# A batched matmul with stores six batches behind the loads, copies of two banks and a small first store

## The chip, the cores and the metric

The kernel runs on one core of a Trainium2 chip. The metric is the device time in microseconds (us), the median of several runs. The profile page describes one execution, and that one has a time of its own.

## The reference

```python
def setup_inputs():
    batch, m, k, n = 16, 512, 512, 512
    return {
        "a": np.random.randn(batch, k, m).astype(np.float32),
        "b": np.random.randn(batch, k, n).astype(np.float32),
    }

def reference(a: np.ndarray, b: np.ndarray) -> np.ndarray:
    return np.matmul(a.transpose(0, 2, 1), b).astype(np.float32)
```

There are 16 independent products of 512x512 matrices, the first one transposed. Each matrix is 1 MB (1,048,576 bytes) in float32, so the kernel must read 32 of them and write 16.

## The kernel before

A batch is one unit of work. Its matrix `a` (512 rows of k by 512 columns of m) lies in SBUF as a tile of 128 partitions, with four consecutive rows of k in each partition. So a partition's part of a batch is one run of 8 KB in memory, and a batch's `a`, `b` and output are each one DMA of 128 such runs. `load(i)` (L45) issues the DMAs of `a` (L46) and `b` (L47), and `store(i)` (L49) the one of the output (L50). All of them are issued by SyncE, SP in the profile, so they stand in one queue.

`compute(i)` (L52) has three steps:

- VectorE (DVE) casts `a` and then `b` from float32 to bfloat16 (L55, L56), 128x2048 each.
- TensorE (PE) makes the output in four groups, one for each `mo`. A group is four matmuls of 128x512 (L61) that are summed in one PSUM bank. The eight banks, `ps0` to `ps7`, are used in turn, so a batch takes four and the next batch the other four.
- ScalarE (ACT) copies each bank to a quarter of the output tile (L68), 128x512 at a time. Its table load before the first copy has the same line.

The buffers are five tiles each of `a` and `b` (`NL`), three of each cast (`NB`), and six output tiles (`NO`), all used in turn. A step that would overwrite a buffer waits until the readers of its former content are done; Tile sets these waits. For its DMAs from SP and ACT, Tile also has eight semaphores that it hands out in turn in the order of the program. A DMA waits until the eighth before it, which had the same semaphore, has landed. So no more than eight are under way at a time.

What sets the order on SP's queue is the loop at the end (L70 to L76): four batches are loaded ahead, and then for each batch come the load of the batch four further on, the computing, and its store. SP issues in that order, and while it waits for one instruction, all behind it wait too. In SP's order the transfers are: ten loads (batches 0 to 4), the store of batch 0, the loads of batch 5, the store of batch 1, and so on. The last load is the 43rd of 48, and the stores of batches 11 to 15 follow it.

Of the kernel before, what the change touches and what calls it, by code (L numbers as in the profile page):

```python
# [1 line left out]

# [4 lines left out]

@with_exitstack
def kernel(
    ctx: ExitStack,  # L10
    tc: tile.TileContext,
    a: bass.AP,
    b: bass.AP,
    out: bass.AP,
):
    nc = tc.nc
    P = 128
    batch, K, M = a.shape
    _, _, N = b.shape
    KO = K // P  # L20
    MO = M // P
    f32 = mybir.dt.float32
    bf = mybir.dt.bfloat16

    a_v = a.rearrange("bat (ki ko) m -> bat ki ko m", ko=KO)
    b_v = b.rearrange("bat (ki ko) n -> bat ki ko n", ko=KO)
    out_v = out.rearrange("bat (mi mo) n -> bat mi mo n", mo=MO)

    LAG = 4
    NL = LAG + 1
    NB = 3
    NO = LAG + 2

    pool = ctx.enter_context(tc.tile_pool(name="sb", bufs=1))
    psum = ctx.enter_context(tc.tile_pool(name="ps", bufs=1, space=bass.MemoryType.PSUM))
    a_ts = [pool.tile([P, KO, M], f32, name=f"a{j}") for j in range(NL)]
    b_ts = [pool.tile([P, KO, N], f32, name=f"b{j}") for j in range(NL)]
    abf_ts = [pool.tile([P, KO, M], bf, name=f"abf{j}") for j in range(NB)]  # L40
    bbf_ts = [pool.tile([P, KO, N], bf, name=f"bbf{j}") for j in range(NB)]
    o_ts = [pool.tile([P, MO, N], f32, name=f"o{j}") for j in range(NO)]
    ps_ts = [psum.tile([P, N], f32, name=f"ps{j}") for j in range(8)]

    def load(i):  # L45
        nc.sync.dma_start(a_ts[i % NL][:], a_v[i])  # L46
        nc.sync.dma_start(b_ts[i % NL][:], b_v[i])  # L47

    def store(i):  # L49
        nc.sync.dma_start(out_v[i], o_ts[i % NO][:])  # L50

    def compute(i):  # L52
        af, bff = abf_ts[i % NB], bbf_ts[i % NB]
        o = o_ts[i % NO]
        nc.vector.tensor_copy(out=af[:], in_=a_ts[i % NL][:])  # L55
        nc.vector.tensor_copy(out=bff[:], in_=b_ts[i % NL][:])  # L56
        a_m = af[:].rearrange("p ko (mi mo) -> p ko mo mi", mo=MO)
        for mo in range(MO):
            pt = ps_ts[(i * MO + mo) % 8]
            for ko in range(KO):  # L60
                nc.tensor.matmul(  # L61
                    pt[:],
                    a_m[:, ko, mo, :],
                    bff[:, ko, :],
                    start=(ko == 0),
                    stop=(ko == KO - 1),
                )
            nc.scalar.copy(out=o[:, mo, :], in_=pt[:])  # L68

    for i in range(min(LAG, batch)):  # L70
        load(i)
    for i in range(batch):
        if i + LAG < batch:
            load(i + LAG)
        compute(i)
        store(i)  # L76


# [1 line left out]
_INS = ['a', 'b']  # L80
_OUTS = [((16, 512, 512), 'float32')]


# [23 lines left out]
```

## Time and profile before

| | |
|---|---|
| Time, median of 5 runs | 126.16 us (125.88 to 126.58) |
| Profiled execution: its time | 126.58 us |
| Profiled execution: its span | 124.9 us |
| PE matmuls (L61) | 76.6 us busy, 61% of the span, 256 of 467 ns in the mean |
| DVE casts (L55, L56) | 39.3 us busy, 31%, 32 of 1227 ns |
| ACT copies (L68) | 37.5 us busy, 64 of 586 ns |
| ACT table load (L68) | 1283 ns, once, starts at 0.7 us |
| First copy of ACT | starts at 11.3 us |
| HBM | 33.55 MB read, 16.78 MB written |
| Transfers of 1 MB, issue to landing | 19.6 us in the median |
| Granted TensorE clock | 0.838 in the mean, 0.5 in some stretches |

The span runs from the first to the last instruction of the profiled execution, and its time is measured around it. A duration under "issue to landing" has in it the time in which a DMA stands in the queue behind others: with seven transfers of some 2.5 us ahead of it, it takes 19.6 us to land though it moves for 2.5. Busy time is no sign of a bound by itself: an engine that is busy a third of the span and never waited for could be slower at no cost.

### The profile page before, as it was taken

How to read it: one execution, taken by the hardware profiler on the slowest of the kernel's cores; microseconds unless marked ns; L12 is line 12 of the kernel's file. 1: busy time of each engine (PE TensorE's matmuls, PEld its weight loads, DVE VectorE, ACT ScalarE, POOL GpSimd, SP SyncE). 2: the span in 40 equal slices, each digit the busy share in tenths (PEclk: the TensorE clock that was granted, in tenths of full speed). 3: DMA queues.
4: the chain of work that ended last, by engine and by line, in shares of the span. 5: the costliest groups of instructions: out<-in, count | busy, mean ns of one | idle time of the engine just before them, and what ended most of it. 6: DMA issues, size and time to landing. Idle time of an engine off the chain costs nothing.

```text
span 124.9 us, 807 instructions
## 1 busy us (share of the span) xinstructions
PE 76.6 (61%) x256; PEld 31.0 (25%) x256; DVE 39.3 (31%) x32; ACT 38.8 (31%) x65; POOL 0.2 (0%) x4
## 2 busy tenths in 40 slices
PE   0009988593709929579470996439397692908920
PEld 0003434242303303123230333113042240402300
DVE  0253455333160330523325042331604333061000
ACT  4001573351701312414170134503315052511220
POOL 0000000000000000000000000000000000000000
PEclk9999999999985595968997569995968779985595
DMA  3999999999999999999999999999999999999945
GB/s 92 425 430 433 425 420 422 422 341 430 422 425 401 417 430 435 420 422 425 425 438 428 422 420 430 433 433 420 422 428 428 433 417 422 425 422 433 401 205 210
DMA packets 6916, 50.38 MB, mean 403 GB/s; under 512 B 768, under 2 KB 768, under 8 KB 768
## 3 DMA queue, kind: packets, MB, share of 16 engines
q1 hardware_dynamic: 6912, 50.33, 96.6%
q8 instruction: 2, 0.03, 0.1%
q14 instruction: 2, 0.02, 0.0%
HBM read 33.55 MB, written 16.78 MB: 403 GB/s over the span
## 4 chain that ended last, share of the span: by engine, by line
DMA 82%; PE 9%; DVE 2%; ACT 1%; issue 0%; SPq 0%; DVEq 0%; ACTq 0%
DMA b<-in_b_dram 38%; DMA out_dram<-o 28%; DMA a<-in_a_dram 16%; PE ps L61 9%; DVE bbf L56 2%; ACT o L68 1%; SPq L46 0%; SPq L47 0%; DVEq L56 0%; ACTq L68 0%; SPq L50 0%
## 5 line engine op out<-in xcount | busy, mean ns | idle before, releaser
L61 PE MATMUL ps<-bbf,abf 128*128 128x512 bf16 x256 | 76.6, 467 | 42.9 <-DVE bbf L56 42.9
L68 ACT COPY o<-ps 128x512 f32<-128x512 f32 x64 | 37.5, 586 | 80.6 <-PE ps L61 80.6
L61 PEld LDWEIGHTS <-abf 128*128 128x128 bf16 x256 | 31.0, 126 | 88.0 <-DVE bbf L56 40.2
L55 DVE CAST abf<-a 128x2048 bf16<-128x2048 f32 x16 | 19.6, 1227 | 52.3 <-DMA a<-in_a_dram 30.0
L56 DVE CAST bbf<-b 128x2048 bf16<-128x2048 f32 x16 | 19.6, 1227 | 21.4 <-DMA b<-in_b_dram 21.4
L68 ACT ACT_TABLE_LOAD x1 | 1.3, 1283 | 0.7 <-PEq L91 0.7
L91 POOL MEMSET const-uint8-127<- 128x1 uint8 x1 | 0.1, 102 | 0.0
L91 POOL MEMSET const-bfloat16-1.0<- 128x1 bf16 x1 | 0.1, 101 | 0.0
L91 POOL MEMSET const-float32-0.0<- 128x1 f32 x1 | 0.1, 99 | 0.2 <-issue 0.2
L91 POOL MEMSET const-float32-1.0<- 128x1 f32 x1 | 0.1, 98 | 0.0
## 6 DMA issues: line engine op xcount, KB each, us to landing
a<-in_a_dram SPq DMA_DIRECT2D x16, 1024.0 KB, 19.6
b<-in_b_dram SPq DMA_DIRECT2D x16, 1024.0 KB, 19.6
out_dram<-o SPq DMA_DIRECT2D x16, 1024.0 KB, 19.6
```

What stands on the lines that cost most here:

```text
L55: nc.vector.tensor_copy(out=af[:], in_=a_ts[i % NL][:])
L56: nc.vector.tensor_copy(out=bff[:], in_=b_ts[i % NL][:])
L61: nc.tensor.matmul(pt[:], a_m[:, ko, mo, :], bff[:, ko, :], start=(ko == 0), stop=(ko == KO - 1),)
L68: nc.scalar.copy(out=o[:, mo, :], in_=pt[:])
L91: nc = _bacc.Bacc("TRN2", target_bir_lowering=False, num_devices=1)
```

## The change

Five things are changed.

- `LAG` is now 6 and no longer the number of batches loaded ahead, which stays at four (`NL - 1`), with five buffers. The store that follows the computing of batch i is that of batch i - 2, so a store stands six batches behind the last load issued before it. The stores that are left over come after the loop. On SP's queue there are now 14 loads ahead of the first store, the last load is the 41st of the 48, and seven stores follow it.
- `NB`, the number of cast buffers, is two instead of three.
- `NO`, the number of output tiles, becomes eight.
- The PSUM tiles are four of two banks each. The matmuls of `mo` 0 and 1 fill the two halves of one, those of `mo` 2 and 3 the next, and ACT copies two banks, 128x1024, with one instruction.
- After the loads of batch 0 have been issued, GpSimd (POOL) fills a 128x128 part of the first output tile with zeros, and ACT issues a DMA of it to the output of batch 0: 128 rows of 512 B, 64 KB. The store of batch 0 writes the same places again later. ACT's first copy writes the same tile, so ACT waits until this DMA has landed; the wait stands before its table load. The DMA takes the second of the eight semaphores in the order of the program.

```diff
-    LAG = 4
-    NL = LAG + 1
-    NB = 3
+    LAG = 6
+    NL = 5
+    NB = 2
     NO = LAG + 2
...
-    ps_ts = [psum.tile([P, N], f32, name=f"ps{j}") for j in range(8)]
+    ps_ts = [psum.tile([P, 2, N], f32, name=f"ps{j}") for j in range(4)]
...
         for mo in range(MO):
-            pt = ps_ts[(i * MO + mo) % 8]
+            pt = ps_ts[(i * MO + mo) // 2 % 4]
             for ko in range(KO):
                 nc.tensor.matmul(
-                    pt[:],
+                    pt[:, mo % 2, :],
                     a_m[:, ko, mo, :],
                     bff[:, ko, :],
                     start=(ko == 0),
                     stop=(ko == KO - 1),
                 )
-            nc.scalar.copy(out=o[:, mo, :], in_=pt[:])
+            if mo % 2:
+                nc.scalar.copy(out=o[:, mo - 1:mo + 1, :], in_=pt[:])
 
-    for i in range(min(LAG, batch)):
+    for i in range(NL - 1):
         load(i)
+        if i == 0:
+
+            nc.gpsimd.memset(o_ts[0][:, 0, 0:P], 0.0)
+            nc.scalar.dma_start(out_v[0][:, 0, 0:P], o_ts[0][:, 0, 0:P])
     for i in range(batch):
-        if i + LAG < batch:
-            load(i + LAG)
+        if i + NL - 1 < batch:
+            load(i + NL - 1)
         compute(i)
+        if i + NL - 1 - LAG >= 0:
+            store(i + NL - 1 - LAG)
+    for i in range(batch + NL - 1 - LAG, batch):
         store(i)
```

## The prediction

> **What bounds the kernel now.** I read the slices of the page first, then the chain of waits in order of time, then the casts in the timeline (each starts when its load has landed), then narrow windows. The engines are out of it: PE is busy 61% of the span, DVE and ACT 31% each. The transfers are not:
>
> ```profile
> DMA  3999999999999999999999999999999999999945
> GB/s 92 425 430 433 425 420 422 422 341 430 422 425 401 417 430 435 420 422 425 425 438 428 422 420 430 433 433 420 422 428 428 433 417 422 425 422 433 401 205 210
> q1 hardware_dynamic: 6912, 50.33, 96.6%
> ```
>
> The reader is to see that 48 transfers of 1 MB leave one queue with hardly a hole: three uneven places, the first slice (92), the ninth (341) and the last two (205, 210). A transfer takes 1.0486 MB / 427 GB/s = 2.455 us (427 is what the window from 44 to 112 us moved). I number the transfers in SP's order, 1 to 48; before, number 43 is the last load and 44 to 48 are stores. The chain has the landings, start plus duration:
>
> ```profile
> 1.16 6.89 DMA b<-in_b_dram
> ...
> 31.23 21.23 DMA b<-in_b_dram
> ...
> 91.90 19.78 DMA b<-in_b_dram
> ...
> 111.78 1.24 DVE bbf L56
> ...
> 113.06 6.39 PE ps L61 x16
> ...
> 119.53 0.58 ACT o L68
> ```
>
> Number 2 lands at 8.05, 19 at 52.46, 43 at 111.68. The end: the last store's issue, and the view of the output's transfers, whose shortest way to landing is that last one:
>
> ```profile
> 120.14 0.33 SPq L50 DMA_DIRECT2D out_dram<-o  x1
> DMA to landing us min/median/max: 3.8/19.6/22.1
> ```
>
> It lands at 123.9; 1.0 us later the span ends, and the run took 126.58, 1.6 more.
>
> **The tail is a trap.** The last two slices are half empty, and the last store visibly waits for cast, matmuls and copy of batch 15 (111.78 to 120.1). But five stores follow load 43, and 111.68 + 5 x 2.455 = 123.96: the measured 123.9. The late store costs next to nothing. The windows show how both can be true:
>
> ```profile
> 118.00:119.00 1.00, 1.00 (x4) 0.40 (x3) 0.00 (x0) 0.54 (x1) 0.00 (x0) 0.68 0.70 295
> 119.00:120.00 1.00, 0.43 (x3) 0.00 (x0) 0.00 (x0) 0.52 (x2) 0.00 (x0) 1.00 0.30 123
> 120.00:121.00 1.00, 0.00 (x0) 0.00 (x0) 0.00 (x0) 0.11 (x1) 0.00 (x0) 1.00 0.23 98
> 121.00:122.00 1.00, 0.00 (x0) 0.00 (x0) 0.00 (x0) 0.00 (x0) 0.00 (x0) 1.00 1.05 442
> ```
>
> The last two columns are the DMA share and GB/s. The share sinks in steps (0.70, 0.30, 0.23): the 16 DMA engines are not abreast. The packet records say that transfer 47 ended on the first engine at 118.3 and on the last at 121.06; a transfer has landed only when its slowest engine is done. The last engine waited 0.14 us for the last store; the idle share belongs to engines that ran ahead. So the end is set by **the most delayed DMA engine**: 48 times its share, plus its stalls.
>
> **Its stalls.** Undisturbed, number 48 would land at 8.05 + 46 x 2.455 = 120.98. It comes 2.9 us later, and 43 is already late by that: 111.68 - (8.05 + 41 x 2.455) = 2.97. Where it was lost, by landings (casts of batches 2, 3 and 4, loads 6, 8, 10):
>
> ```profile
> 18.01 1.23 DVE L56 CAST bbf<-b 128x2048 bf16<-128x2048 f32 x1 [1.25 <-DMA b<-in_b_dram]
> ...
> 23.04 1.23 DVE L56 CAST bbf<-b 128x2048 bf16<-128x2048 f32 x1 [1.21 <-DMA b<-in_b_dram]
> ...
> 28.74 1.23 DVE L56 CAST bbf<-b 128x2048 bf16<-128x2048 f32 x1 [1.95 <-DMA b<-in_b_dram]
> ```
>
> Two transfers should take 4.91: the step to 23.04 took 5.03, the next 5.70, a loss of **0.79**. From 28.74 to 52.46 nine transfers should take 22.10 and took 23.72: **1.62**. From there to 111.68: 0.30. Before 23.04: 0.24. Sum 2.95. The 0.79 in windows:
>
> ```profile
> 26.00:27.00 1.00, 1.00 (x7) 0.50 (x5) 0.79 (x1) 0.59 (x2) 0.00 (x0) 1.00 0.92 319
> 27.00:28.00 1.00, 0.97 (x5) 0.29 (x3) 0.00 (x0) 0.59 (x1) 0.00 (x0) 1.00 0.92 303
> ...
> 40.00:41.00 1.00, 1.00 (x4) 0.29 (x2) 0.00 (x0) 0.22 (x1) 0.00 (x0) 0.50 0.91 336
> ```
>
> In the packet records an 8 KB packet takes 309 ns, but 45 packets between 25.5 and 28.2 took up to 621, two at 32.6 and nine near 40 (up to 971). These three places lie some 2 us ahead of the first packet of the first, second and third store (27.4, 34.8, 42.2); the 13 later stores have none. The first load has the like: its first packets took 1.1 to 1.3 us, b's first load had two long ones, later loads none. So these look like costs of the first uses of a tensor by the engines, paid as descriptors are taken in; that is my reading, not shown. The third place is an instruction fetch of 16 KB at 42.6, which held one engine 0.98 us. [...]
>
> **The change, part by part.**
>
> *Stores later.* In SP's built order number 15 is the first store (was 11), the last load is 41 (was 43), and seven stores follow it. Store i is issued after the load of batch i+6, so SP waits for no copy that isn't long done. The chain after load 41 (at about 105) is 1.24 + 6.39 + at most 1.2 + 0.1 = 9 us; six stores before the last give 14.7 us of cover. Gain: 0 to 0.14, I take 0.04. Loads keep their order and their five buffers: a load waits for the cast five batches before and for the eighth transfer before it, as now. Seven pairs of loads now run ahead of stores, 4.9 us a batch, against PE's 3.65 (full clock) to 6.9 (16 matmuls 0.43 apart, as at the clock of 0.5 in the last batch): even at 6.9, PE falls behind by 2 us a batch over seven batches, some 12 us, and store 5 (number 30), issued when 22 lands at about 57, finds batch 5 done at 14.7 + 5 x 6.9 = 49. No stall. Pure stores ran at 426 GB/s from 112 to 118, so a longer tail of them costs nothing.
>
> *Two cast buffers.* The cast of batch j waits for PE of j-2 instead of j-3. With 7.4 us a batch (three transfers) and PE at most 6.9 it waits little; behind it on DVE stand only later casts, and the loads have about 7 transfers of cover. 0; if the cover went, one cast pair, 2.5 us, would be added to a batch.
>
> *Copies of two banks.* 64 x 586 ns become 32 at between 586 and 1172 ns; I take 1.0 us. ACT is busy 31% of the span: 0. Only the last copy could count, 0.4 us, under the same cover.
>
> *The small store.* POOL fills 128x128 (the page has only 128x1 fills, 0.1 us; up to some 5 us it would delay nobody, as follows); ACT issues 64 KB (SP's issues take 0.33 to 0.65); the first copy and its table load (1.28) now wait for its landing. The first copy was due at 11.3 and with two banks at 13: landing at even 6 leaves 5 us. It takes one of eight DMA semaphores: load 8 waits for load 1 (5.6 instead of 4.29), with 12 us of queue before it: 0. The wire: 0.0655 MB / 427 = 0.15 by bytes; 8 packets an engine at a full packet's 309 ns would be 2.5. [...] Ends: -0.1 to 2.5.
>
> *What it may take away.* It touches the whole of batch 0's output, from all engines, while the first loads still wait for their first bytes (33 GB/s in the first 2 us). If the stalls ahead of the first stores are first uses, 0.79 and about 0.3 (near 40) go or fall into that gap. Ends: 0 and 1.6 (with what is unplaced of the 1.62, less the fetch). I take 1.1.
>
> Sum: -0.04 + 0.15 - 1.1 = -1.0. The profiled run (126.58) is the highest of five; the median is 126.16, and what scatters is this same delay, so I subtract from the median: **125.1**; from the profiled run it would be 125.6.
>
> **Rivals.**
> 1. *The stalls stay*, ahead of number 15 instead of 11, or are paid at the start: +0.15 - 0.04: 126.3. For it: half of the engines lost more than the others, which first use doesn't explain. Chance 0.30.
> 2. *Slower: small packets cost like large ones*, 128 writes of 512 B wedged between the first loads on each engine: from 0.09 us a packet (0.7 an engine), with nothing taken away, it is over 0.5%; at 0.2 us 127.7. [...] Chance 0.13.
> 3. *The plain reading of the tail*: the 3.2 us missing in the last two slices come back: 123. Against it: 111.68 + 12.28. Chance 0.05.
>
> **Numbers.** Forecast 0.52, its own range 124.5 to 125.6. The range 124.3 to 126.5 takes in rival 1 and leaves out 3 and most of 2. A measurement here tells 0.5%, 0.63 us, from nothing: below 125.53 is faster. Faster: 0.50 of the forecast, rival 3, and 0.03 of rival 1: 0.58. Same: 0.28. Slower: 0.14.
>
> **What would show it.** No dip like 303 to 319 GB/s ahead of the first store (now near 36 us), loads landing 2.46 apart; last load at about 105; the last store issued under running stores; the small store landed before 6 us; the most delayed engine still carrying a fetch of 1 us. Wrong: the same dip moved, a hole after 2 us, or an end well before the sum of 2.455 us steps.

## The result, and the profile after

The change makes no difference to the time that can be measured. The changed kernel takes 126.3 us in the median (125.85 to 126.79), the kernel before, over all its 80 runs beside it, 126.54; the ratio is 0.9996, with a 95% interval of 0.9981 to 1.001. That is the first rival's time, not the forecast 125.1. Runs more than 1.5% above the fastest of their kernel are left out of all ratios; the stores on ACT's queue and the quarters, further on, have two each. One thing did change: the 80 times of the kernel before lie in two heaps (30 below 126.2 us, 46 above 126.4), those of the changed kernel in one between them, and their standard deviation is 0.24 us instead of 0.51. So a median of few runs of the kernel before, such as the 126.16 from which the prediction subtracted, depends on how many fell into which heap. What parts the heaps is open, as no execution from the lower one was profiled. The profiled execution took 126.44 us with a span of 124.7, against 126.58 and 124.9.

The page's slices of the changed kernel, DMA share and GB/s:

```profile
DMA  3999999999999999999999999999999999999991
GB/s 84 423 423 423 431 431 423 423 421 421 423 410 418 394 423 431 410 431 431 415 426 431 426 428 428 423 426 428 426 426 431 415 431 426 423 428 426 423 381 42
```

The two half-empty slices at the end are gone: 381 and 42 where 205 and 210 stood. The hole in the ninth slice is gone from there, and shallower ones stand in the twelfth and fourteenth (410, 394). The time has not followed either. The parts whose cost was estimated have rows of their own now (groups and DMA issues of the page):

```profile
L69 ACT COPY o<-ps 128x1024 f32<-128x1024 f32 x32 | 32.4, 1013 | 73.0 <-PE ps L61 62.6
...
out_dram<-o ACTq DMA_DIRECT2D x1, 64.0 KB, 5.1
```

A copy of two banks takes 1013 ns (estimated 1.0 us) and nobody waits for it. The small store is issued at 0.96 and lands 5.1 us later; ACT's table load starts at 6.10, long before the first copy is due. But the second load lands at 8.35 instead of 8.05: this landing came 0.30 later, not 0.15.

The end of the chain of waits, and the tail in windows of 1 us (last columns: DMA share, GB/s):

```profile
106.76 1.24 DVE bbf L56
...
108.05 3.66 PE ps L61 x16
...
111.78 1.01 ACT o L69
```

```profile
119.00:120.00 1.00, 0.00 (x0) 0.00 (x0) 0.00 (x0) 0.00 (x0) 0.00 (x0) 0.50 0.97 410
120.00:121.00 1.00, 0.00 (x0) 0.00 (x0) 0.00 (x0) 0.00 (x0) 0.00 (x0) 0.50 0.93 393
121.00:122.00 1.00, 0.00 (x0) 0.00 (x0) 0.00 (x0) 0.00 (x0) 0.00 (x0) 0.50 0.49 205
122.00:123.00 1.00, 0.00 (x0) 0.00 (x0) 0.00 (x0) 0.00 (x0) 0.00 (x0) 0.50 0.12 49
```

The reader is to see that computing ends at 112.8, more than ten microseconds before the end, and that nothing in the last stretch waits for an engine: DMA engines finish one after another. In the records of landings, the last store is complete on the first DMA engine at 121.11, on the last but one at 123.38 and on the last at 123.74. Before, the first engine completed it at 123.84 and the last at 123.98.

Where the slowest engine lost its time can be read from the casts, as before. The casts of batches 5, 6 and 7 in the timeline (loads 12, 14 and 16; store number 15 stands between the last two):

```profile
33.30 1.23 DVE L56 CAST bbf<-b 128x2048 bf16<-128x2048 f32 x1 [1.23 <-DMA b<-in_b_dram]
...
38.95 1.23 DVE L56 CAST bbf<-b 128x2048 bf16<-128x2048 f32 x1 [1.90 <-DMA b<-in_b_dram]
...
45.36 1.23 DVE L55 CAST abf<-a 128x2048 bf16<-128x2048 f32 x1 [5.19 <-DMA a<-in_a_dram]
```

Two transfers should take 4.91 us. The first pair took 5.65, the second 6.41: losses of **0.74** and **1.50**. The first is the stall that stood ahead of store number 11 before (0.79) and has moved with the first store to number 15: its long packets (up to 592 ns) now lie between 35 and 38 us.

```profile
35.00:36.00 1.00, 1.00 (x6) 0.54 (x5) 0.18 (x1) 0.00 (x0) 0.00 (x0) 1.00 0.92 377
```

The dip is shallower than the 319 and 303 GB/s before, as fewer packets are long (13 over 370 ns against 34), but the slowest engine loses as much. In the second loss lies a fetch of 16 KB of instructions at 39.2 us. It took 0.93 us, and the data packet behind it 716 ns instead of 309; in the records of landings the last engine falls from 0.69 us behind the last but one to 1.96 behind it, so about 1.27 of the 1.50 are the fetch. From there on the transfers land in step: 48 lands at 123.74, within 0.1 of number 15's landing (42.80) + 33 x 2.455. So from the second load on the sum is 8.35 + 46 x 2.455 + 2.46 = 123.74, where before it was 8.05 + 46 x 2.455 + 3.0.

### The profile page after: what moved, and what is told of

It is laid out like the page before. It is cut to its first block, busy times and chain, and to the rows that moved or that the text cites. A ratio compares the mean times of both kernels' runs of the same rounds, so it can differ in the third digit from the quotient of the medians.

```text
span 124.7 us, 756 instructions
## 1 busy us (share of the span) xinstructions
PE 69.1 (55%) x256; PEld 29.7 (24%) x256; DVE 39.3 (31%) x32; ACT 33.7 (27%) x33; POOL 0.4 (0%) x5
## 4 chain that ended last, share of the span: by engine, by line
DMA 84%; PE 3%; DVE 1%; ACT 1%; issue 0%; SPq 0%; DVEq 0%; ACTq 0%
DMA a<-in_a_dram 35%; DMA b<-in_b_dram 33%; DMA out_dram<-o 16%; PE ps L61 3%; DVE bbf L56 1%; ACT o L69 1%; SPq L47 0%; DVEq L56 0%; ACTq L69 0%; SPq L50 0%; SPq L46 0%
## 5 line engine op out<-in xcount | busy, mean ns | idle before, releaser
L61 PE MATMUL ps<-bbf,abf 128*128 128x512 bf16 x256 | 69.1, 431 | 42.6 <-DVE bbf L56 42.5
L69 ACT COPY o<-ps 128x1024 f32<-128x1024 f32 x32 | 32.4, 1013 | 73.0 <-PE ps L61 62.6
L61 PEld LDWEIGHTS <-abf 128*128 128x128 bf16 x256 | 29.7, 121 | 81.5 <-DVE bbf L56 39.5
```

The costliest lines, as they stand in the source:

```text
L61: nc.tensor.matmul(pt[:, mo % 2, :], a_m[:, ko, mo, :], bff[:, ko, :], start=(ko == 0), stop=(ko == KO - 1),)
L69: nc.scalar.copy(out=o[:, mo - 1:mo + 1, :], in_=pt[:])
```

## The experiments

All ratios are to the kernel before, run on the same chip beside each. Theory A, from the prediction, says that the most delayed DMA engine sets the end and that stores and tail are off the path. Theory B is the plain rival: the later stores gain and the small store takes it back. The base of some runs is the changed kernel without its small store, as in the first one; it is called the plain base.

### Parts alone

The changed kernel without its small store:

```diff
-        if i == 0:
-
-            nc.gpsimd.memset(o_ts[0][:, 0, 0:P], 0.0)
-            nc.scalar.dma_start(out_v[0][:, 0, 0:P], o_ts[0][:, 0, 0:P])
```

> The changed kernel without the small store. Theory A (the end is set by the most delayed DMA engine, and the small store costs the first loads 0.3 us): some 0.3 us less than the changed kernel, 0.2 to 0.3% below the kernel before; the stall ahead of the first store (some 0.7 us of spread between first and last engine) stays. Theory B (the later stores gain about 1 us and the small store takes it back): 0.8% or more below before.

Measured: 1.0006 (0.9985 to 1.0026), 126.62 us. B is out: it needed 0.992. But A's 0.997 to 0.998 lies outside the interval as well: the 0.30 us that the small store puts on the second load's landing are not gained back without it. The stall ahead of number 15 is there without the small store too, as expected, if smaller in this execution: the first and the last engine land number 13 0.43 us apart and number 14 0.72, and eight packets ahead of number 15 took up to 841 ns. (At number 15 they are 2.06 apart; that is mostly the fetch at 38.6.)

The changed kernel with the old distance of the stores:

```diff
-    LAG = 6
+    LAG = 4
...
-    NO = LAG + 2
+    NO = 8
```

> The changed kernel with the stores four batches behind the loads as before (eight output tiles kept). Theory A: as the changed kernel within 0.2 us, though the last two slices go half empty again. Theory B: slower than the changed kernel by about 1 us, 0.8% above before.

Measured: 0.9997 (0.9965 to 1.0028). So in the median two batches more or less between loads and stores are worth nothing within 0.3%, and B falls a second time. The scatter goes with the distance here, for a reason that no run shows: the standard deviation is 0.56 us here and 0.47 in the next run, both with stores four batches behind, against 0.24 for the changed kernel. One expectation missed: in the profiled execution the tail is not half empty (its last two slices move 428 and 122 GB/s). There the matmuls of the last batch took 3.64 us (3.65 in the kernel before at 24.33 us, where its windows show a granted clock of 1.00) instead of 6.37 (clock 0.56 over them), so the last store was in the queue in time. In these two profiles the hole in the tail goes with the time of one batch's matmuls, and the medians do not show it.

The kernel before with the small store alone:

```diff
     for i in range(min(LAG, batch)):
         load(i)
+        if i == 0:
+
+            nc.gpsimd.memset(o_ts[0][:, 0, 0:P], 0.0)
+            nc.scalar.dma_start(out_v[0][:, 0, 0:P], o_ts[0][:, 0, 0:P])
```

> The kernel before with the small store alone. Theory A: 0.3 us more than before, 0.2%; the stall ahead of the first store stays where it was, 2 us ahead of transfer 11. Theory B: about 1 us more, 0.8%. The prediction's step (the small store takes the stalls of the first stores away) would make it 0.8 us less.

Measured: 1.0013 (0.9989 to 1.0038): not the -0.8 us of the prediction's step, and A's +0.3 lies within. A window of it, where the stall of the kernel before stood:

```profile
26.00:27.00 1.00, 1.00 (x6) 0.55 (x5) 1.00 (x1) 0.72 (x2) 0.00 (x0) 1.00 0.96 328
27.00:28.00 1.00, 1.00 (x7) 0.45 (x4) 0.12 (x1) 0.72 (x2) 0.00 (x0) 1.00 1.07 377
```

328 and 377 GB/s against 319 and 303: the small store has been written twenty microseconds earlier, and the stall is in its place, with 27 packets over 370 ns against 34.

### The fetch

One matmul of each group of four, so that the sums lack three quarters of their terms:

```diff
-            for ko in range(KO):
+            for ko in range(1):
...
-                    stop=(ko == KO - 1),
+                    stop=(ko == 0),
```

> The changed kernel with one of the four matmuls of each group, so that three quarters of the products are left out and PE has 128 instead of 512 instructions; no 16 KB instruction fetch should be left in the trace. Theory A: the most delayed engine loses its 0.9 us of fetch, so the last and the first engine end a transfer at most 1.5 us apart instead of 2.45, and the time is 0.7 to 1.0 us below the changed kernel. If the most delayed engine does not set the end, the time does not move, since PE is not on the path.

Measured: 125.96 us, 0.9964 (0.9945 to 0.9983), so 0.45 us below the kernel before, and about 0.4 below the changed kernel by the two ratios. The queues of its page, with the row that the changed kernel has besides:

```profile
q1 hardware_dynamic: 6912, 50.33, 97.0%
q10 hardware_dynamic: 144, 0.07, 0.2%
q14 instruction: 2, 0.02, 0.0%
...
q8 instruction: 2, 0.03, 0.1%
```

The row q8, the two fetches of 16 KB, is gone. PE, which lost three quarters of its work, was on no path before, so the gain comes through the transfers. The fetch is the likely cause, but not shown to be the only one: in this execution the stall ahead of the first store is nearly gone too (one packet, 493 ns), and the granted clock was 1.0. The gain is half of what was expected, since other stalls take the fetch's place: the landings lose 0.75 us at numbers 15 and 16 and 0.6 at number 29, and at the end the engines are 1.95 us apart instead of 2.63.

### What the stall ahead of the first store is

Theory D says first use of the output by each engine, theory C says a common passage from loads to stores. First, a whole store of zeros as the third transfer, in place of the small one:

```diff
+    nc.gpsimd.memset(o_ts[0][:], 0.0)
     for i in range(NL - 1):
         load(i)
         if i == 0:
-
-            nc.gpsimd.memset(o_ts[0][:, 0, 0:P], 0.0)
-            nc.scalar.dma_start(out_v[0][:, 0, 0:P], o_ts[0][:, 0, 0:P])
+            store(0)
```

> The changed kernel, with the small store replaced by a full store of 1 MB of zeros to batch 0's output as the third transfer. One transfer more: 2.46 us. Theory D (the stalls are first uses of the output by the engines, which 64 KB did not cover): no stall ahead of the first true store, spread of the engines under 1.5 us, and about 1.3 to 1.8 us more than the changed kernel. Theory C (engines that pass from loads to stores together hold each other up until they are spread over about one transfer): the spread comes anyway, and the time is 2.3 to 2.6 us above the changed kernel, some 129.0.

Measured: 130.09 us, 1.0286 (1.0222 to 1.0349), 3.8 us above the changed kernel: one transfer (2.46) and 1.3 more. Its windows, early and then ahead of the first true store (number 16, whose packets begin at 40.4 us):

```profile
6.00:7.00 1.00, 0.00 (x0) 0.11 (x1) 0.78 (x1) 0.00 (x0) 0.00 (x0) 1.00 1.09 287
7.00:8.00 1.00, 0.00 (x0) 0.00 (x0) 0.00 (x0) 0.00 (x0) 0.00 (x0) 1.00 1.03 229
8.00:9.00 1.00, 0.00 (x0) 0.00 (x0) 0.00 (x0) 0.00 (x0) 0.00 (x0) 1.00 0.82 287
...
39.00:40.00 1.00, 1.00 (x6) 0.55 (x5) 0.41 (x1) 0.00 (x0) 0.00 (x0) 1.00 0.98 410
```

The stall came early, and dearer (229 to 287 GB/s for three microseconds), and between 14 and 42 us, where the fetch comes, no packet took over 330 ns. So in this run the stall came with the *full* store, at the front, and the first true store behind it has none. It is not paid once for all, though: ahead of the sixth true store, between 75.4 and 77.0 us, 15 packets took up to 662 ns. Neither theory had the time right: C is 1.2 to 1.5 us short, D 2.0 to 2.5. And 64 KB don't take the stall away. Nor do 16 rows of 8 KB, one full packet for each engine:

```diff
-            nc.gpsimd.memset(o_ts[0][:, 0, 0:P], 0.0)
-            nc.scalar.dma_start(out_v[0][:, 0, 0:P], o_ts[0][:, 0, 0:P])
+            nc.gpsimd.memset(o_ts[0][0:16], 0.0)
+            nc.scalar.dma_start(out_v[0][0:16], o_ts[0][0:16])
```

> The changed kernel with the small store made of 16 rows of 8 KB (128 KB, one packet for each engine) instead of 128 pieces of 512 B. Theory D with full packets as the first use: no stall 2 us ahead of transfer 15, 0.3 us for the packets, so 0.3 to 0.6 us less than before. If one packet an engine is not enough, or the stall belongs to the passage from loads to stores: the stall stays, 0.2 to 0.4 us more than before.

Measured: 0.9987 (0.9972 to 1.0002), between the two forecasts, so that the trace has to decide: the long packets at 36 to 38 us are there (up to 888 ns), and the slowest engine loses 0.7 us.

These numbers are of one profiled execution each, and they differ: at the landing ahead of the first store the slowest engine lost 0.75 us in the kernel before, 0.70 in the changed one, 0.5 in the kernel before with the small store, 0.4 without it or with the old distance, and nothing with one matmul a group. Later stores have stalls too. Ahead of the first six stores there are 34, 2, 9, 0, 0 and 0 packets over 370 ns in the kernel before, 13, 8, 6, 3, 0 and 0 in the changed one, and 24, 3, 6, 4, 11 and 2 with the old distance.

The plain base with all stores but the last left out:

```diff
-        if i + NL - 1 - LAG >= 0:
-            store(i + NL - 1 - LAG)
-    for i in range(batch + NL - 1 - LAG, batch):
+    for i in range(batch - 1, batch):
         store(i)
```

> The changed kernel without the small store, with all stores left out but the last, so that 15 of the 16 products are never written. Both theories say that the stalls come with stores: the engines should stay within 0.6 us of each other through the loads, except for the one that serves the 16 KB fetch (1.0 us more). If loads alone spread them to 2 us, stores are not the cause. About 94 to 97 us.

Measured, in one run: 96.86 us. The engines land their loads 0.46 us apart up to number 13; then the fetch at 38 us holds one engine 1.06 us, the data packet behind it takes 812 ns instead of 309, and from there the spread is 1.74: one fetch set this engine back 1.25 us. A second one, at 79 us and of 1.10, does not add to the spread, so it seems to have met another engine. No load is held up otherwise. So in these runs the stalls come with the stores, and the fetches come on top.

### Attempts at something faster

Theory C also said that stalls stop once the engines are spread over one transfer. It rested on a misreading: the ends of packets had been sorted by time and cut into groups of sixteen, and once an engine is more than a transfer behind, such groups mix transfers and can't show more than one transfer's length. The landings of each transfer by itself show 2.85 us in the kernel before, and 2.63 after. The runs that were made for it tell other things. The plain base with transfers of half the columns:

```diff
-        nc.sync.dma_start(a_ts[i % NL][:], a_v[i])
-        nc.sync.dma_start(b_ts[i % NL][:], b_v[i])
+        for h in (slice(0, 2), slice(2, 4)):
+            nc.sync.dma_start(a_ts[i % NL][:, h], a_v[i][:, h])
...
```

> The changed kernel without the small store, each load and store in two transfers of 128 partitions and half of the columns of a partition (4 KB a packet, 96 transfers). Theory C (stalls go on until the engines are spread over one transfer): a spread of about 1.2 to 1.4 us at the end and 0.8 to 1.1 us less than before. Theory D (first uses and fetches, whatever the size of a transfer): spread of 1.7 to 2.5 us and the time of before within 0.4 us.

Measured: 129.95 us, 1.0274 (1.0238 to 1.031), and a true spread of 3.3 us: C falls. A packet of 4 KB takes 159 ns, two 318, against 309 for one of 8 KB: 9 ns on each of 384 packets of 8 KB an engine are 3.5 us, about what was lost (3.4); what the larger spread adds is not told apart from that. D, which allowed 0.4 us, misses as well.

Halves, and quarters in the same way, by partitions instead:

```diff
+        for h in range(2):
+            r = slice(h * P // 2, (h + 1) * P // 2)
+            nc.sync.dma_start(a_ts[i % NL][r], a_v[i][r])
...
```

> The changed kernel without the small store, each load and store in two transfers of 64 partitions. Theory C: the engines are spread over one transfer of half the size, 1.2 to 1.4 us instead of 2.45, and the time falls by 0.8 to 1.1 us (ratio 0.992). Theory D: the spread and the time stay (within 0.3 us), or the time grows by what 48 more transfers cost.

> The same in four transfers of 32 partitions. Theory C: a spread of about 1 us, which the 16 KB instruction fetch alone holds up, and 1.0 to 1.6 us less than before (ratio 0.988 to 0.992), unless eight transfers of 256 KB under way are too few. Theory D: no less than the changed kernel.

Measured: 194.81 us (1.5402, 1.5323 to 1.5482) and 199.8 (1.5783, 1.5685 to 1.5882). Nothing that either theory allowed for; see the last section.

The plain base with stores on ACT's queue, beside the loads on SP's:

```diff
-        nc.sync.dma_start(out_v[i], o_ts[i % NO][:])
+        nc.scalar.dma_start(out_v[i], o_ts[i % NO][:])
```

> The changed kernel without the small store, with all stores issued by ACT on a second queue, so that each DMA engine has packets of loads and stores side by side. Theory C: no common switch, spread below 1.5 us, 0.5 to 1.0 us less than the changed kernel. Theory D: the first uses stall as before, no less time.

Measured: 1.0189 (1.0134 to 1.0244), from runs of 128.4 to 129.16 us. A window where the first store's packets begin (20.8 us), and windows of the end:

```profile
20.00:21.00 1.00, 1.00 (x7) 0.49 (x6) 0.34 (x1) 0.24 (x1) 0.00 (x0) 1.00 0.92 270
...
112.00:115.00 3.00, 2.73 (x13) 1.50 (x14) 1.44 (x2) 1.11 (x2) 0.00 (x0) 1.00 1.01 423
115.00:118.00 3.00, 1.70 (x9) 0.71 (x7) 1.23 (x1) 1.25 (x2) 0.00 (x0) 1.00 0.57 240
118.00:121.00 3.00, 2.86 (x14) 1.25 (x12) 0.00 (x0) 1.12 (x2) 0.00 (x0) 1.00 0.76 309
121.00:124.00 3.00, 0.00 (x0) 0.00 (x0) 0.00 (x0) 0.91 (x1) 0.00 (x0) 1.00 0.41 175
```

The stall is there with stores on a queue of their own: 56 packets between 19.4 and 23.4 us took up to 713 ns. The end is what an exposed tail looks like. Stores no longer stand behind loads, so they take their turns early, and the last load lands near 115.8 instead of 106.7. The last two stores can only be issued when ACT has copied their batches, at 117.0 and 121.9, and in between all engines idle, not those ahead alone: they land the last store within 0.16 us of each other. Compare the tail of the kernel before, where five stores were left.

Last, loads of two batches in one transfer of 2 MB, with runs of 16 KB (rows dealt to other partitions) and of 8 KB:

```diff
-    a_v = a.rearrange("bat (ki ko) m -> bat ki ko m", ko=KO)
+    a_v = a.rearrange("(j two) k m -> j (two k) m", two=2).rearrange("j (ki ko) m -> j ki ko m", ko=2 * KO)
...
-        if i + NL - 1 < batch:
-            load(i + NL - 1)
+        if i % 2 == 0 and i // 2 + NP - 1 < batch // 2:
+            load(i // 2 + NP - 1)
```

> The changed kernel without the small store, loads of two batches in one transfer of 2 MB with 16 KB runs; the rows are dealt to the partitions otherwise than the product needs, so the output is another one, with the same instructions. If what a packet costs beyond its bytes (4 KB took 159 ns, 8 KB 309, so 9 ns) is saved on half of the packets of the loads: 128 packets less an engine, 1.1 us less than before (ratio 0.991). If 16 KB packets take twice 309: no less. The spread tells whether it stops at one transfer: then it can pass 2.45 us while 2 MB transfers run.

> The same transfers of 2 MB with runs of 8 KB, rows dealt as the product needs. No packet is saved: the time of before within 0.4 us. If the slowest engine's own stalls set the end, the end follows the last packet of the slowest engine by 1.3 us, as in all runs so far, whatever the spread is; if the spread stops at one transfer, it can pass 2.45 us.

Measured: 1.0014 (0.9991 to 1.0037) and 1.006 (1.0039 to 1.0082). A packet of 16 KB takes 611 ns, 7 less than two of 309: by 128 packets 0.9 us less. None of it shows in the time, and the engines are 3.5 us apart by the end; that it is lost there is argued, not shown. The second, at 0.5 to 1.0 us more than before, misses its 0.4 us, and why is open. Of the versions that do all of the work, none is below the kernel before by more than its interval.

## Why the prediction failed

*What bounds the kernel: right.* Transfers set the time, and in them the slowest DMA engine. In the profiles of the changed kernel, without its small store, with the old distance, with one matmul a group, and with the 16 rows, the first engine lands the last store between 120.94 and 121.37, and the last one between 123.06 and 123.75. The kernels' times in those same executions (125.77 to 126.46) are the last engine's landing and 2.7 to 3.0 us, and they rank as the last engine's landings do.

*The tail is a trap: right, but narrowly.* The last two slices filled up and gave nothing back (rival 3 said 123), and two kernels that differ in this distance alone are alike within 0.3% in the median. In the kernel before the late last store, with its 6.37 us of matmuls ahead of it, came down on the first engine at 123.84, only 0.14 before the slowest engine was through: had the stalls gone there, the tail would have set the end.

*Two cast buffers, copies of two banks: right*, no cost seen; the copy's size was estimated to 1%.

*The small store: right in kind, small in size.* The sum's 0.15 us are its bytes at 427 GB/s, the author's estimate; no run shows them as a cost. What the runs show is a second load that landed 0.30 later (8.35 against 8.05), and no gain that can be measured from leaving the store out (1.0006, 0.9985 to 1.0026). Its packets were cheap: in the records of the changed kernel each of the 128 packets of 512 B took 27 ns, 0.22 us for the eight of an engine, where the upper end of 2.5 put 309 and rival 2 needed 90 or more. It landed 5.1 us after its issue, with nobody waiting.

*"What it may take away", 1.1 us: wrong*, and this is the step that failed. The prediction read long packets ahead of the first three stores as first uses of the output that any touch would settle, and priced them as gone. That the stalls need stores held in the run with one store. But 64 KB that reach all 128 rows of batch 0's output from all engines don't take them away, nor do full packets on 16 rows: the first one moved with the first full store (0.74 against 0.79), and about 1.27 of the second loss (1.50) is the fetch, which the prediction rightly left in place, but put at about 1 us, from the 0.98 for which one engine was held in the kernel before. So the term was worth nothing instead of 1.1, and what is left is near rival 1, to which 0.30 was given. That its 126.3 was met to the decimal is luck: it was counted from 126.16, and the kernel before stood at 126.54 this time. Half of the engines losing more than the others, named there as speaking against a first use, should have weighed more.

Open: what the DMA engines wait for ahead of the first stores. A first use of more of the output than was touched does not by itself explain the 15 long packets ahead of the sixth store behind the store of zeros. A passage from loads to stores in one queue does not explain the stall with the stores on a queue of their own. That the stalls end when the engines are far enough apart fits the traces of the kernel before and of the changed one (behind the fourth store the only packets over 370 ns are three in each, of 582 to 787 ns, that start as a fetch of instructions ends), but no run tests it.

## What to carry to other kernels

Here all loads and full stores went through one queue and kept the DMA engines busy, and the end was that of the slowest engine (123.98 us before, 123.74 after). In a kernel like it, take the landing of the last load, add the transfers behind it, and compare with the end before believing an empty-looking tail. A stall whose cause is read from where it stands is not one that a cheap measure removes; price its removal by a run that removes it, and until then as a rival. Instruction fetches counted as transfers here (one set a DMA engine back 1.25 us in the run with one store): where transfers are the bound, fewer instructions on an engine that waits all day may still shorten the kernel, as the run with one matmul a group suggests (0.45 us below the kernel before). And look at all times of a kernel, not at the median alone, before subtracting from it.

## What was not expected of the hardware

Loads in transfers of 64 partitions ran at half the rate in this case. A window of the halves by partitions, from its loads:

```profile
10.00:40.00 30.00, 18.18 (x48) 6.36 (x47) 7.36 (x6) 5.32 (x6) 0.00 (x0) 0.77 1.02 218
```

All sixteen DMA engines are busy (share 1.02) and move 218 GB/s instead of 425 (the kernel before, from 4 to 25 us, at a share of 1.01); their 8 KB packets take about 610 ns instead of 309. What they wait for no run shows. Two halves in turn don't make up for it (194.81 us for the kernel), nor do four transfers of 32 partitions (199.8).

A fetch of 16 KB of instructions took 0.9 to 1.1 us beside full transfers (0.93 and 0.98 in the changed kernel, 1.06 and 1.10 in the run with one store), half again and more what two data packets of 8 KB take (0.62), and in the loads of the run with one store that alone, with the slow packet behind it, made the difference between engines 0.46 and 1.74 us apart.
